# A two-layer hybrid encoder trunk: longer allowances in the clock that orders attention and projection work

## Chip, core and metric

The kernel runs on one core of one Trainium2 chip. A core has a matrix engine (TensorE, PE in the profile; PEld is its weight load), a vector engine (VectorE, DVE), an engine for activation functions and scaled copies (ScalarE, ACT), a general engine (GpSimd, POOL) and an engine that here issues the transfers (SyncE, SP). Each takes its own instructions strictly in the order in which the program lists them, and waits at an instruction until what it needs is there. The metric is the time of one execution on the device in microseconds, as the median of several runs.

## What is computed

Two layers over 512 tokens of width 1024. The attention of each layer has two branches that matter here, eight heads each: latent attention ("mla") and grouped-query attention ("gqa", eight query heads over two key heads of width 64).

```python
for l in range(DEPTH):                      # DEPTH = 2, SEQ = 512, D_MODEL = 1024
    h = rms_norm(x, attn_norm_g[l])
    proj = h @ w_in[l]
    c_q, c_kv, k_rope, gq, gk, gv, pool_in, gate_logits = split_columns(proj, IN_SIZES)
    o_mla = mla_branch(c_q, c_kv, k_rope, ...)      # 8 heads, keys of width 96, values of 64
    o_gqa = gqa_branch(gq, gk, gv, ...)             # 8 heads over 2 key heads, width 64
    o_pool = pool_branch(pool_in, pool_w[l], pool_scale[l])
    gates = sigmoid(gate_logits).reshape(b, s, 3, d)
    merged = (gates[:, :, 0] * (o_mla @ w_branch_mla[l])
              + gates[:, :, 1] * (o_gqa @ w_branch_gqa[l])
              + gates[:, :, 2] * (o_pool @ w_branch_pool[l]))
    x = x + merged @ w_out[l]
    hf = rms_norm(x, ffn_norm_g[l])
    u = depthwise_conv(hf @ ffn_w_up[l], ffn_conv_w[l], ffn_conv_b[l])
    x = x + (silu(u[..., :D_FF]) * u[..., D_FF:]) @ ffn_w_down[l]
```

Each head does `softmax(q k^T / sqrt(d)) v`.

## The kernel before

Everything stays on one core, and activations lie feature by feature: 128 features of all 512 tokens are one tile. A product in float32 is made of three matmuls on rounded halves (`mm3`): high by high, high by low, low by high. A 512-wide matmul of a 128x128 block is the unit of PE's work.

**Filler.** The gate and branch projections and the latent heads' own projections are cut into pieces of three or more matmuls. A `Filler` hands them out one by one (`fill.step()`), always in the same order. They need little from other engines, so they are put between the steps of the heads, which wait for other engines often.

**Banks.** PSUM is cut into eight banks: two each for `acc`, `ST` and `AV`, one each for `S` and `mi`. Taking one is `ps(tag)`, giving it back is `free(tag)`, which notes the time from which it counts as free.

**The ordering clock.** The program's order is not written down by hand. While it is being written out, a small clock (`Clock`, object `ck`) keeps a time for every engine from estimated costs: `ck.now` is the time at which PE stands, `ck.ready[key]` the time from which a result counts as there, and the numbers in `banks[tag]` those from which a bank is free. No such time is in the finished program; they decide only which instruction is listed next. On the chip, semaphores do the waiting, whatever the clock thought.

**Grouped-query heads** (`PLAN["gqa"]`). A fixed plan gives each step of the eight heads a place in the stretch of filler. The steps of a head are: `t_q` (its queries are cut into high and low), four `s_max` (a rough score block, 128 queries by 512 keys, in the single bank `S`, whose row maximum DVE takes; the bank is free when DVE has read it), four `probs` (the scores that are used, from two matmuls into a bank `ST` or `mi`, then exponential on ACT, high and low parts on ACT and DVE, and a partial sum on DVE, after which the bank is free), then `av_hi`, `av_lo` and `av_rest` (the product with the values). Before a step is listed, filler is listed up to the place that the plan gives, and after that more filler, piece by piece, as long as `waiting` says that a key or bank of the step is not there yet, to at most `SLACK` = 35 pieces ahead of the place.

**Latent heads** (`held_banks`). Here a list of tasks is gone through again and again, and the first that may go is listed (`can`); if none may, a piece of filler is. `a_part` makes a score block's first matmul into any bank that `sc_ready` finds free, and DVE takes its maximum (`largest`); after the fourth, DVE joins the maxima and writes a row of them (`row`) into the operand `qb`, which counts as key `m`. `b_part` adds the two other matmuls, the second of which reads `qb`, and the exponential follows. A task's `margin` is how long its keys must have been there by the clock.

In the listings below, `ps_S<-ka,qa` is an `s_max`, `ps_ST<-qa,ka` and `ps_ST<-qb,kb` (or `ps_mi`) a `probs`, `ps_AV<-ph`, `<-pl` and `<-vt` the three products with the values, `ps_ST<-qa,kh` (or `mi`, `S`, `AV`) an `a_part`, `<-qa,kl` and `<-qb,kh` a `b_part`, and `ps_acc` filler.

Of the kernel before, what the change touches and what calls it, by code (L numbers as in the profile page):

```python
# [60 lines left out]
D_OUT, D_IN, D_LAT = 3.2, 4.0, 6.0  # L61
D_FREE, D_SUM = 0.8, (2.0, 0.8)
REST = 0.4
GAP = 3.0
ONLY = True
HOLD = (0.65, 0.15)
# [93 lines left out]
class Clock:  # L160
# [49 lines left out]
    def done(self, *key):  # L210
        self.ready[key] = self.fin + self.SEM
# [10 lines left out]
    def chain(self, *steps, after=0.2):  # L222

        def go(n, source=None, since=None):
            if n == len(steps):
                return
            keys, fn = steps[n] if isinstance(steps[n], tuple) else ((), steps[n])
            late = [self.ready.get(k, self.now + 0.5) for k in keys]
            if late and max(late) > self.now:
                self.at(max(late) - self.now, lambda: go(n))  # L230
                return
            if fn in self.waits and self.pause[0] <= self.now < self.pause[1] - 0.001:
                self.at(self.pause[1] - self.now, lambda: go(n, source, since))
                return
            eng, most = self.gives_way.get(fn, (None, 0.0))
            since = self.now if since is None else since
            if self.free.get(eng, 0.0) > self.now + 0.02 and self.now < since + most:
                self.at(self.free[eng] - self.now, lambda: go(n, source, since))
                return
            self.fin, self.source, self.last = self.now, source, None  # L240
            fn()
            source, self.source = self.last, None
            self.at(max(0.0, self.fin - self.now), lambda: go(n + 1, source))
        self.at(after, lambda: go(0))
# [74 lines left out]
def trunk(ctx: ExitStack, tc: tile.TileContext, x, w, prm, gb, cst, pad, out):  # L319
    nc = tc.nc  # L320
    ctx.enter_context(tc.manual_schedule())
    ck = Clock()
# [30 lines left out]
    banks = {k: [0.0] * n for k, n in nbank.items()}  # L353
# [172 lines left out]
    for l in range(L):  # L526
        t = cp.tile([P, NPRM], F32, tag=f"prm{l}", name=f"prm{l}")
        prms.append(t)

    def split(hi, lo, src, scale=None, eng=None):  # L530

        steps = []
        if scale is None:
            steps.append(lambda: A.activation(hi, src, AF.Copy))
            steps.append(lambda: (eng or V).tensor_tensor(lo, src, f(hi), ALU.subtract))
        else:
            steps.append(lambda: A.activation(hi, src, AF.Copy, scale=scale))
            steps.append(lambda: V.scalar_tensor_tensor(lo, src, scale, f(hi), ALU.mult, ALU.subtract))
        return steps
# [128 lines left out]
    def layer(l, sq, xsrc):  # L668
# [616 lines left out]
        def attention(kind, fill, okey, odst):  # L1285
            gqa = kind == "gqa"
            hs, ot = {}, []

            def key(*k):
                return (kind, l) + k  # L1290
# [3 lines left out]
            def sc_tags():  # L1294
                return ("ST", "mi", "S") + ("AV",) * (held[0] == 0)

            def sc_ready():
                return any(banks[t] and banks[t][0] <= ck.now for t in sc_tags())

            def sc_bank():  # L1300
                while not any(banks[t] for t in sc_tags()):
# [288 lines left out]
            def held_banks():  # L1590
                todo = []

                def task(fn, *args, keys=(), margin=0.2, bank=None, after=(), fills=0.0):
                    todo.append((fn, args, keys, margin, bank, after, fills))

                lead, late = LEAD[kind]
                step = (fill.total - fill.done - late) / 7.0
                f0 = fill.done
                issued = set()
                for h in range(8):  # L1600
                    if not gqa and h + 1 < 8 or gqa and h in (1, 3, 5):
                        n = h + 1
                        task(go_turn, n, after=[(a_part, h - 1, 3)] if not gqa and h else [(a_part, h, 0)] if gqa else ())
                    q = [("gqn", l, b) for b in range(4)] if gqa and h == 0 else [("tp" if gqa else "tq", l, h)]
                    if not gqa or h % 2 == 0:
                        task(t_q, h, keys=q, bank="mi" if gqa and h == 0 else None, after=[(a_part, h - 1, 3)] if h else ())
                    if not gqa:
                        task(t_k, h, keys=[("tk", l, h)], after=[(t_q, h)])
                    for k in range(4):
                        task(a_part, h, k, keys=[key("q" if gqa else "qh", h)] + [key("kh", h)] * (not gqa), margin=0.1, bank="sc",  # L1610
                             after=[(t_q, h - h % 2 if gqa else h)] + [(b_part, h - 1, 3)] * (h > 0) + [(t_k, h)] * (not gqa)
                             + [(a_part, h, k - 1)] * (k > 0), fills=f0 + step * h if k == 0 else 0)
                    for k in range(4):
                        task(b_part, h, k, keys=[key("m", h), key("q", h)] + [key("kl", h)] * (not gqa), margin=0.4,
                             after=[(b_part, h, k - 1) if k else (a_part, h, 3)])
                    for k in range(4):
                        task(av_hi, h, k, keys=[key("ph", h, k)], margin=lead, bank="AV" if k == 0 else None,
                             after=[(av_hi, h, k - 1) if k else (b_part, h, 0), (b_part, h, k)] + [(av_rest, h - 1)] * (h > 0))
                        task(av_lo, h, k, keys=[key("pl", h, k)], margin=lead,
                             after=[(av_hi, h, k)])  # L1620
                    task(av_rest, h, keys=[key("t", h, 3)], margin=lead, after=[(av_lo, h, k) for k in range(4)])

                def can(fn, args, keys, margin, bank, after, fills):
                    if not all(x in issued for x in after):
                        return False
                    if fills and fill.done < min(fills, fill.total):
                        return False
                    if not all(ck.ready.get(k, 1e9) + margin <= ck.now for k in keys):
                        return False
                    if bank == "sc":  # L1630
                        return sc_ready()
                    return not bank or bool(banks[bank]) and banks[bank][0] <= ck.now

                while todo:
                    for n, z in enumerate(todo):
                        if can(*z):
                            todo.pop(n)
                            z[0](*z[1])
                            issued.add((z[0],) + z[1])
                            break  # L1640
                    else:
                        if not fill.step():
                            ck.to(ck.now + 0.05)
                fill.finish()
# [6 lines left out]
            for h in range(8):  # L1651
# [4 lines left out]
                for k in range(4):  # L1656
                    plan += [(p0 + s0 + ds * k, s_max, (h, k)), (p0 + 4 + k, probs, (h, k)),
                             (p0 + 4 + k + ah, av_hi, (h, k)), (p0 + 4 + k + al, av_lo, (h, k))]
                plan.append((p0 + 7 + al + REST, av_rest, (h,)))
            plan.sort(key=lambda z: z[0])  # L1660
# [4 lines left out]
            def waits(fn, h, k=None):  # L1665

                if fn is go_turn:
                    return [], None
                if fn is t_q:
                    if gqa and h == 0:  # L1670
                        return [("gqn", l, b) for b in range(4)], "mi"
                    return [] if gqa and h % 2 else [("tp" if gqa else "tq", l, h)], None
                if fn is t_k:
                    return [("tk", l, h)] * (not gqa), None
                if fn is s_max:
                    return [key("q", h)] + [key("kh", h)] * (not gqa), "S"
                if fn is probs:
                    return [key("m", h), key("q", h)] + [key("kl", h)] * (not gqa), ("ST", "mi")
                if fn is av_hi:
                    return [key("ph", h, k)], "AV" if k == 0 else None  # L1680
                return [key("t", h, 3)] if fn is av_rest else [key("pl", h, k)], None

            def waiting(fn, *args):
                keys, tag = waits(fn, *args)
                tags = (tag,) if isinstance(tag, str) else tag or ()
                return not ck.has(*keys) or bool(tags) and not any(banks[t] and banks[t][0] <= ck.now for t in tags)

            f0, first = fill.done, plan[0][0]
            for pos, fn, args in plan:
# [51 lines left out]
        tags = ("acc", "ST", "AV", "mi", "S")  # L1741
# [212 lines left out]
        def again(k):  # L1954

            turned[k] = [slot("tf", F32R)[:, :T] for _ in range(4)]
            for i, (src, hi, lo, key_) in enumerate((
# [3 lines left out]
                SY.dma_start(t, src)  # L1961
                chain(*split(hi, lo, t, eng=G), lambda key_=key_: done(*key_), after=D_IN + GAP * i + 3.0 * (k == 0))

# [312 lines left out]
```

## Time and profile before

| what | value |
|---|---|
| time, median of 3 runs | 1524.32 us (1524.0 to 1524.4) |
| the profiled execution's own time | 1525.42 us |
| its span, from first to last instruction | 1523.6 us, 25155 instructions |
| read from HBM, written | 159.89 MB, 22.02 MB |
| layer 0: grouped-query heads, latent heads | 104 to 216 us, 218 to 343 us |
| layer 1: the same | 860 to 972 us, 974 to 1098 us |

The last two rows are stretches of the trace that hold those heads; the rest of a layer is projections and the feed-forward part. Three kinds of view are used below: the busy time of each engine in a stretch, what PE's weight load waited for, and the timeline of an engine, in which a row's first two numbers are its start and its length in us. Matmuls overlap in the pipeline: a row is longer than the distance from its start to the next one's, and it is this distance that tells how fast PE goes. What stands between brackets is idle time that even the overlap doesn't hide.

### The profile page before, as it was taken

To read this page: it belongs to the slowest core of one execution; us is meant where nothing else is said; L and a number is where in the kernel's file an instruction comes from. 1 tells how busy PE (TensorE), PEld (TensorE's weight loads), DVE (VectorE), ACT (ScalarE), POOL (GpSimd) and SP (SyncE) were. 2 spreads that over 40 slices of the span, in tenths; PEclk is the share of its full clock that TensorE was granted. 3 is DMA by queue.
4 is the path that set the end of the run, shared out by engine and by line. 5 is a ranking of instruction groups with operands and counts; after the bars stand their busy time and mean duration, and the time that the engine had idled before them with its cause. 6 is when DMAs were issued, how large, how long until landed. Compare 5 with 4: busy or idle time off the path is not lost.

```text
span 1523.6 us, 25155 instructions
## 1 busy us (share of the span) xinstructions
PE 1513.9 (99%) x8390; PEld 1326.5 (87%) x8390; DVE 1188.6 (78%) x2375; ACT 980.0 (64%) x1973; POOL 1121.2 (74%) x1076
## 2 busy tenths in 40 slices
PE   9999999999999999999999999999999999999998
PEld 8888788788889899999998888888888899989998
DVE  5778989985578885778857789899855788867786
ACT  6468876664567675666654688676636676756763
POOL 4865986865689897676778659868547897977664
PEclk9999999999999999999999999999999999999999
DMA  6432234424244453233435322444243444533232
GB/s 219 116 116 79 66 106 139 130 88 148 96 136 145 149 185 110 92 101 108 140 127 135 101 77 67 124 132 133 78 152 97 142 149 139 182 109 100 96 114 95
DMA packets 91954, 183.56 MB, mean 120 GB/s; under 512 B 21936, under 2 KB 43696, under 8 KB 91824
## 3 DMA queue, kind: packets, MB, share of 16 engines
q1 hardware_dynamic: 91680, 181.94, 37.9%
q8 instruction: 66, 1.08, 0.3%
q14 instruction: 64, 0.52, 0.1%
q10 hardware_dynamic: 144, 0.01, 0.0%
HBM read 159.89 MB, written 22.02 MB: 119 GB/s over the span
## 4 chain that ended last, share of the span: by engine, by line
PE 89%; DVE 5%; ACT 2%; issue 1%; DMA 1%; POOL 1%; SPq 0%; DVEq 0%; POOLq 0%; ACTq 0%
PE ps_acc L497 29%; PE ps_AV L497 18%; PE ps_ST L497 10%; PE ps_ST L1927 10%; PE ps_acc L1927 9%; PE ps_AV L1927 7%; PE ps_S L497 2%; PE ps_mi L497 2%; DVE nmt L295 1%; DVE vt L289 1%; DVE pl L285 1%; PE ps_ST L1467 1%; DMA tf<-pad 0%; DVE ph L303 0%; ACT wh L277 0%
## 5 line engine op out<-in xcount | busy, mean ns | idle before, releaser
L285 POOL TENSOR_TENSOR wl<-raw,wh 128x512 fp32r<-128x512 f32 (+3 forms) x500 | 594.1, 1197 | 288.0 <-ACT wh L277 236.5
L277 ACT ACTIVATE wh<-raw 128x512 fp32r<-128x512 f32 (+2 forms) x521 | 291.2, 577 | 18.1 <-PE ps_ST L497 10.4
L497 PE MATMUL ps_acc<-HH,wh 128*128 128x512 f32 x504 | 197.0, 391 | 0.0
L497 PE MATMUL ps_acc<-HL,wh 128*128 128x512 f32 x504 | 196.5, 390 | 0.0
L497 PE MATMUL ps_acc<-HH,wl 128*128 128x512 f32 x504 | 196.4, 390 | 0.0
L497 PEld LDWEIGHTS ps_acc<-HH,wl 128*128 128x128 f32 x504 | 94.6, 188 | 20.0
L497 PEld LDWEIGHTS ps_acc<-HL,wh 128*128 128x128 f32 x504 | 94.7, 188 | 19.1
L497 PEld LDWEIGHTS ps_acc<-HH,wh 128*128 128x128 f32 x504 | 94.7, 188 | 18.9 <-DVE gt L285 0.6
L497 PE MATMUL ps_AV<-HH,wh 128*128 128x512 f32 x248 | 96.7, 390 | 0.0
L497 PE MATMUL ps_AV<-HL,wh 128*128 128x512 f32 x248 | 96.6, 390 | 0.0
L497 PE MATMUL ps_AV<-HH,wl 128*128 128x512 f32 x248 | 96.6, 389 | 0.0
L277 ACT ACTIVATE wh<-ps_S 128x512 fp32r<-128x512 f32 x79 | 47.1, 597 | 40.4 <-DVE ps_S L285 28.6
L277 ACT ACTIVATE wh<-ps_mi 128x512 fp32r<-128x512 f32 x79 | 47.1, 596 | 38.4 <-DVE ps_mi L285 32.4
L285 DVE TENSOR_TENSOR wl<-ps_mi,wh 128x512 fp32r<-128x512 f32 x79 | 54.1, 685 | 11.4 <-ACT wh L277 10.8
L285 POOL TENSOR_TENSOR a<-a,cv 128x511 f32<-128x511 f32 x36 | 46.1, 1294 | 22.6 <-DVE a L289 22.6
L285 DVE TENSOR_TENSOR wl<-ps_S,wh 128x512 fp32r<-128x512 f32 x79 | 54.1, 685 | 9.9 <-ACT wh L277 9.3
L1927 PE MATMUL ps_ST<-ah,wh 128*128 128x256 f32 x298 | 59.8, 283 | 0.2 <-ACT wh L277 0.2
L277 ACT ACTIVATE gt<-gt 128x512 f32<-128x512 f32 x48 | 30.2, 628 | 43.5 <-DVE gt L285 43.1
L497 PEld LDWEIGHTS ps_AV<-HH,wl 128*128 128x128 f32 x248 | 46.6, 188 | 9.8
L1927 PE MATMUL ps_acc<-ah,wh 128*128 128x256 f32 x276 | 55.0, 283 | 0.0
L497 PEld LDWEIGHTS ps_AV<-HH,wh 128*128 128x128 f32 x248 | 46.6, 188 | 9.3
L497 PEld LDWEIGHTS ps_AV<-HL,wh 128*128 128x128 f32 x248 | 46.6, 188 | 9.3
(583 smaller groups left out, 5173.4 us busy)
## 6 DMA issues: line engine op xcount, KB each, us to landing
raw<-w SPq DMA_DIRECT2D x228, 512.0 KB, 3.6
raw<-w SPq DMA_DIRECT2D x13, 384.0 KB, 3.0
XM<-x SPq DMA_DIRECT2D x16, 256.0 KB, 3.2
back<-hsp SPq DMA_DIRECT2D x16, 256.0 KB, 4.1
back<-tsp SPq DMA_DIRECT2D x16, 256.0 KB, 4.4
dtq<-tr SPq DMA_DIRECT2D x16, 192.0 KB, 1.9
dtk<-tr SPq DMA_DIRECT2D x16, 192.0 KB, 2.0
tf<-dtq SPq DMA_DIRECT2D x48, 64.0 KB, 2.0
```

The costliest lines, as they stand in the source:

```text
L277: return self.eng.activation(out, in_, func, **k)
L285: return self.eng.tensor_tensor(out, *a)
L289: return self.eng.scalar_tensor_tensor(out, *a)
L295: return self.eng.tensor_reduce(out, in_, *a, **k)
L497: PE.matmul(o, lhsT=lhsT, rhs=rhs, start=start, stop=stop)
L1467: PE.matmul(sc, lhsT=s[a_][:, kb_], rhs=s[b_][:, :T], start=False, stop=n == len(pairs) - 1, skip_group_check=True)
L1927: PE.matmul(banks_[b][1][:, 256 * at_:256 * at_ + 256], lhsT=(his, his, los)[q][i][:, ws], rhs=right[n][q == 1], start=first and b not in ...
```

## The change

Three conditions get longer allowances, all of them in the ordering clock.

```diff
+LATE = (0.3, 0.3)
...
             def sc_ready():
-                return any(banks[t] and banks[t][0] <= ck.now for t in sc_tags())
+                return any(banks[t] and banks[t][0] + 0.5 <= ck.now for t in sc_tags())
...
                     for k in range(4):
-                        task(b_part, h, k, keys=[key("m", h), key("q", h)] + [key("kl", h)] * (not gqa), margin=0.4,
+                        task(b_part, h, k, keys=[key("m", h), key("q", h)] + [key("kl", h)] * (not gqa), margin=0.8,
...
             def waiting(fn, *args):
                 keys, tag = waits(fn, *args)
                 tags = (tag,) if isinstance(tag, str) else tag or ()
-                return not ck.has(*keys) or bool(tags) and not any(banks[t] and banks[t][0] <= ck.now for t in tags)
+                return any(ck.ready.get(k, 1e9) + LATE[0] > ck.now for k in keys) or \
+                    bool(tags) and not any(banks[t] and banks[t][0] + LATE[1] <= ck.now for t in tags)
```

In the grouped-query heads a step's keys and bank count as there only 0.3 us after the time that the clock has for them. In the latent heads a bank for `a_part` counts as free 0.5 us after, and the keys of `b_part` must have been there for 0.8 us instead of 0.4.

On PE both programs have the same instructions. Filler moves to earlier places and the heads' steps to later ones, by 24 matmuls at most, inside the two stretches of each layer; the last product of the last head of each kind stands behind the same amount of filler in both. Three places follow.

The first is on PE, in layer 0's grouped-query heads, between the first and the second `s_max` of head 6 (operands `qa_2071` before, `qa_2104` now). Before, the end of that piece:

```order
L497 MATMUL ps_AV_2041<-ph_2035,vg_591 128x512
L497 MATMUL ps_AV_2041<-pl_1950,vg_589 128x512
L497 MATMUL ps_acc_2057<-HH,wh_2013 128x512
L497 MATMUL ps_acc_2057<-HL,wh_2013 128x512
L497 MATMUL ps_acc_2057<-HH,wl_2014 128x512
L497 MATMUL ps_S_2148<-ka_595,qa_2071 128x512
```

and now its end:

```order
L498 MATMUL ps_acc_2203<-opl_919,wh_2038 128x512
L498 MATMUL ps_acc_2203<-oph_918,wl_2039 128x512
L498 MATMUL ps_acc_2203<-oph_925,wh_2038 128x512
L498 MATMUL ps_acc_2203<-opl_926,wh_2038 128x512
L498 MATMUL ps_acc_2203<-oph_925,wl_2039 128x512
L498 MATMUL ps_acc_2203<-oph_934,wh_2038 128x512
L498 MATMUL ps_acc_2203<-opl_935,wh_2038 128x512
L498 MATMUL ps_acc_2203<-oph_934,wl_2039 128x512
L498 MATMUL ps_acc_2203<-oph_952,wh_2038 128x512
L498 MATMUL ps_acc_2203<-opl_953,wh_2038 128x512
L498 MATMUL ps_acc_2203<-oph_952,wl_2039 128x512
L498 MATMUL ps_S_2227<-ka_595,qa_2104 128x512
```

Between the two `s_max` stood two products with the values and 6 filler matmuls; now it is the same two products and 15 filler matmuls.

The second is on PE, in layer 0's latent heads, where the last score block of head 3 is taken between the products with the values of head 2. Before:

```order
L497 MATMUL ps_AV_3209<-ph_3176,vm_2545 128x512
L1425 MATMUL ps_mi_3224<-qa_3088,kh_3091 128x512
L497 MATMUL ps_AV_3209<-pl_3170,vm_2543 128x512
L1425 MATMUL ps_S_3228<-qa_3088,kh_3091 128x512
L1425 MATMUL ps_AV_3231<-qa_3088,kh_3091 128x512
L1425 MATMUL ps_ST_3234<-qa_3088,kh_3091 128x512
```

and now:

```order
L498 MATMUL ps_AV_3212<-pl_3171,vm_2539 128x512
L1426 MATMUL ps_AV_3239<-qa_3091,kh_3094 128x512
L498 MATMUL ps_acc_3241<-oh_1775,wh_3098 128x512
L498 MATMUL ps_acc_3241<-ol_1776,wh_3098 128x512
L498 MATMUL ps_acc_3241<-oh_1775,wl_3099 128x512
L498 MATMUL ps_AV_3212<-pl_3177,vm_2541 128x512
L498 MATMUL ps_acc_3241<-oh_2116,wh_3098 128x512
L498 MATMUL ps_acc_3241<-ol_2117,wh_3098 128x512
L498 MATMUL ps_acc_3241<-oh_2116,wl_3099 128x512
L1426 MATMUL ps_ST_3256<-qa_3091,kh_3094 128x512
```

The four `a_part` of head 3 stood nearly together; now 7 other matmuls stand between the third and the fourth alone.

The third is on DVE, the chain of maxima of the same head 3 (the four `nmt` of 128x16 are the maxima of the four blocks, `mrow` and `qb` end the chain). Before:

```order
L295 TENSOR_REDUCE nmt_3226<-ps_mi_3224 128x16
L289 SCALAR_TENSOR_TENSOR vt_3191<-ps_ST_3080,vm_131_1030,vt_3191 128x512
L295 TENSOR_REDUCE nmt_3226<-ps_S_3228 128x16
L295 TENSOR_REDUCE nmt_3226<-ps_AV_3231 128x16
L295 TENSOR_REDUCE nmt_3226<-ps_ST_3234 128x16
L295 TENSOR_REDUCE nmt_3226<-nmt_3226 128x16
L311 STREAM_TRANSPOSE osum_2967<-oinv_3124 128x512
L295 TENSOR_REDUCE nmt_3226<-nmt_3226 32x16 x3
L285 TENSOR_TENSOR gt_3260<-ps_acc_3135,rbc_374 128x512
L295 TENSOR_REDUCE mrow_3271<-nmt_3226 32x16
L285 TENSOR_TENSOR qb_3089<-mrow_3271,C 32x512
```

and now:

```order
L296 TENSOR_REDUCE nmt_3222<-ps_AV_3239 128x16
L290 SCALAR_TENSOR_TENSOR vt_3200<-ps_ST_3083,vm_131_1030,vt_3200 128x512
L286 TENSOR_TENSOR gt_3237<-ps_acc_3134,rbc_374 128x512
L312 STREAM_TRANSPOSE osum_2967<-oinv_3127 128x512
L296 TENSOR_REDUCE nmt_3222<-ps_ST_3256 128x16
L296 TENSOR_REDUCE nmt_3222<-nmt_3222 128x16
L296 TENSOR_REDUCE nmt_3222<-nmt_3222 32x16 x3
L296 TENSOR_REDUCE mrow_3293<-nmt_3222 32x16
L290 SCALAR_TENSOR_TENSOR gt_2689<-gt_2689,ps_acc_3241 128x512
L286 TENSOR_TENSOR qb_3092<-mrow_3293,C 32x512
```

The transpose of `osum` and the gate's `gt<-ps_acc` stood inside the chain, behind the fourth maximum; now they stand ahead of it, and another piece of the gates stands ahead of `qb`.

## The prediction

> **What bounds the kernel now.** I read the page first, for the engine that sets the end.
>
> ```profile
> PE 1513.9 (99%) x8390; PEld 1326.5 (87%) x8390; DVE 1188.6 (78%) x2375; ACT 980.0 (64%) x1973; POOL 1121.2 (74%) x1076
> PEclk9999999999999999999999999999999999999999
> ```
>
> PE is busy for 99% of the span at the full granted clock. The change adds and removes no matmul, so it can win only what PE now waits, and lose only by new waits. Next come the four stretches that hold the heads, as busy time by engine.
>
> ```profile
> core 0: us, PE busy (x) PEld busy (x) DVE busy (x) ACT busy (x) POOL busy (x), PEclk, DMA share, GB/s
> 104.00:216.00 112.00, 110.86 (x506) 91.30 (x505) 96.70 (x175) 87.70 (x174) 82.81 (x114) 1.00 0.23 75
> 218.00:343.00 125.00, 124.32 (x550) 101.69 (x549) 114.85 (x211) 81.35 (x152) 87.70 (x75) 1.00 0.42 125
> 860.00:972.00 112.00, 111.17 (x507) 91.66 (x506) 96.30 (x176) 89.22 (x175) 81.83 (x113) 1.00 0.23 75
> 974.00:1098.00 124.00, 123.67 (x546) 100.89 (x545) 114.68 (x211) 80.53 (x152) 86.78 (x74) 1.00 0.42 127
> ```
>
> PE's plain idle time there is 1.14 + 0.68 + 0.83 + 0.33 = 3.0 us. That is too little, since a matmul's row lasts longer than its turn, and a short wait hides under the row before. The reader is to see also that DVE is the second engine: 86% in the first and third stretch, 92% in the others. The waits show fully at the weight load, which stands ahead of each matmul. Of the view of waits over the whole span, with the engine PEld, these rows belong to the heads' stretches:
>
> ```profile
> PEld ps_S L497 <- DVE nm L295: 4.7, 8, 1.0
> PEld ps_ST L1425 <- DVE vt L289: 2.0, 4, 0.7
> PEld ps_acc L497 <- DVE gt L285: 1.8, 4, 0.6
> PEld ps_mi L1467 <- DVE qb L285: 0.7, 1, 0.7
> PEld ps_acc L497 <- DVE XM L289: 0.7, 2, 0.4
> PEld ps_acc L497 <- ACT MQ L277: 0.6, 1, 0.6
> PEld ps_S L497 <- ACT qb L277: 0.4, 1, 0.4
> PEld ps_AV L1467 <- DVE qb L285: 0.3, 1, 0.3
> PEld ps_ST L1467 <- DVE qb L285: 0.2, 1, 0.2
> ```
>
> The columns are total us, times, longest. The largest group is a rough score block that waits for the only bank `S`, because DVE has not yet read the block before (`nm`). The next is a latent score block that waits for a bank which DVE's partial sum `vt` still reads, and the three `qb` rows are score parts that wait for the row of maxima. What such a wait costs is read from one of the two longest.
>
> ```profile
> 178.91 0.39 PE L497 MATMUL ps_acc<-HH,wl 128*128 128x512 f32 x1
> 179.86 0.50 PE L497 MATMUL ps_S<-ka,qa 128*128 128x512 f32 x1 [0.56 <-DVE nm L295]
> 180.20 0.39 PE L497 MATMUL ps_ST<-qa,ka 128*128 128x512 f32 x1
> ...
> 176.10 2.39 DVE L285 TENSOR_TENSOR qa<-tf,qa 64x512 fp32r<-64x512 f32 x2
> 178.52 0.69 DVE L295 TENSOR_REDUCE ssm<-mns 128x8 f32<-128x512 f32 x1
> 179.13 0.68 DVE L295 TENSOR_REDUCE nm<-ps_S 128x1 f32<-128x512 f32 x1
> ```
>
> The usual pitch is taken where nothing waits:
>
> ```profile
> 130.85 0.39 PE L497 MATMUL ps_ST<-qa,ka 128*128 128x512 f32 x1
> ...
> 132.90 0.39 PE L497 MATMUL ps_acc<-oph,wh 128*128 128x512 f32 x1
> ```
>
> From the first to the last of these rows are nine matmuls: 2.05 / 9 = 0.23 us each. At 179.86 the distance is 0.95, so 0.72 is lost, and the next distance is 0.34, so 0.11 more: 0.83 us, where the weight load's wait is 1.0 (the longest of its group). I take 0.83 of a weight-load wait as its cost. The `S` group then costs 4.7 x 0.83 = 3.9 us, `vt` and `qb` together 3.2 x 0.83 = 2.7, and the four groups that remain 3.5 x 0.83 = 2.9.
>
> **The change part by part.** No semaphore, transfer or tile size is changed. The three conditions move filler forward and steps back, so each edit's price is a cover longer or shorter by so many matmuls of 0.23 us.
>
> Grouped-query heads, 0.3 more for keys and banks. The clock moves in pieces of three matmuls, 0.68 us, so a step that was just due gets one piece or more. I looked up the eight places of the `S` group in both orders. At four the cover grows. In head 6 of either layer it goes from 8 to 17 matmuls, 2.0 us more than the 0.83 that was lost. At 127.77 it goes from 8 to 11 and at 155.79 from 8 to 14 (six of them 256 wide, so about 0.7 us more):
>
> ```profile
> 126.99 0.39 PE L497 MATMUL ps_acc<-HH,wl 128*128 128x512 f32 x1
> 127.77 0.50 PE L497 MATMUL ps_S<-ka,qa 128*128 128x512 f32 x1 [0.39 <-DVE nm L295]
> 128.10 0.39 PE L497 MATMUL ps_mi<-qa,ka 128*128 128x512 f32 x1
> ...
> 155.26 0.39 PE L497 MATMUL ps_acc<-oph,wl 128*128 128x512 f32 x1
> 155.79 0.50 PE L497 MATMUL ps_S<-ka,qa 128*128 128x512 f32 x1
> 156.13 0.40 PE L497 MATMUL ps_mi<-qa,ka 128*128 128x512 f32 x1
> ...
> 934.46 0.39 PE L497 MATMUL ps_acc<-HH,wl 128*128 128x512 f32 x1
> 935.41 0.50 PE L497 MATMUL ps_S<-ka,qa 128*128 128x512 f32 x1 [0.57 <-DVE nm L295]
> ```
>
> The losses there are 0.55 + 0.10 = 0.65, then 0.30 + 0.11 = 0.41, and 0.72 + 0.11 = 0.83 in layer 1. With the first 0.83 that is 2.7 us, less than the added cover at each place, and I count it as gone. At the other four places the cover stays within 0.05 us of what it was; their 3.9 - 2.7 = 1.2 us stays. At four places that are not among the eight (the second gap of head 4, and in layer 1 the third gap of head 1 and the last two of head 4) the cover shrinks by three matmuls, 0.68. That costs between nothing and 0.68 at each; since none of them waited, some of the cover was spare, and I take a third, 0.23, together +0.9 us.
>
> Latent heads, banks 0.5 later and `b_part` at 0.8. Their waits look like these:
>
> ```profile
> 269.42 0.39 PE L1425 MATMUL ps_AV<-qa,kh 128*128 128x512 f32 x1
> 270.06 0.50 PE L1425 MATMUL ps_ST<-qa,kh 128*128 128x512 f32 x1 [0.26 <-DVE vt L289]
> 270.40 0.39 PE L497 MATMUL ps_acc<-HH,wh 128*128 128x512 f32 x1
> ...
> 276.81 0.40 PE L1467 MATMUL ps_mi<-qa,kl 128*128 128x512 f32 x1
> 277.44 0.50 PE L1467 MATMUL ps_mi<-qb,kh 128*128 128x512 f32 x1 [0.23 <-DVE qb L285]
> 277.77 0.40 PE L1467 MATMUL ps_S<-qa,kl 128*128 128x512 f32 x1
> ...
> 275.59 1.79 DVE L285 TENSOR_TENSOR qb<-mrow,C 32x512 fp32r<-32x512 f32 x1
> ```
>
> They lose 0.41 + 0.11 and 0.40 + 0.10 us. In the new order 7 matmuls, 1.6 us, stand ahead of that fourth score block, and two long pieces have left its chain of maxima, for one that came in. The parts are spread, so three of the four maxima are taken before the last block comes, while from the fourth block to `b_part` the distance hardly changes (4.8 to 6.1 us of matmuls now, 4.8 to 6.4 before). An allowance of 0.5 covers a wait of 0.5, and the longest here is 0.7 at the weight load. I count 80% of 2.7 as gone: -2.1 us; the bounds are none of it and all of it.
>
> Not addressed: the waits for `gt`, `XM`, `MQ` and ACT's `qb`, 2.9 us. They are waits for an `acc` bank or a copy that no allowance looks at. They fall anew with another order, up or down, and I take nothing. Filler at earlier places also needs its weights earlier, by up to 24 matmuls or 5.4 us. The projections outside the heads take weights at PE's full pace all along, and the heads' stretches hold filler for only part of the time, so I price it at nothing; if POOL and ACT failed to keep up, it would show as a wait for `wh` or `wl`, up to the 1.8 us of the largest group that is not addressed. The transfers are the same 594, a few in another order. Both kinds of heads end behind the same matmul as before, so the stages behind them move by the sum and no more.
>
> The sum: -2.7 + 0.9 - 2.1 = -3.9 us. The profiled execution would go from 1525.4 to 1521.5 us, its span from 1523.6 to 1519.7. It lies 1.1 us above the median of the runs, to which I apply the same step: 1524.3 - 3.9 = **1520.4 us**.
>
> **The rivals.** First, the waits come back elsewhere, because the clock's errors are longer than the allowance. Behind 179.86 and 277.44 stand two DVE pieces with both inputs in SBUF that took far longer than usual, as the view by tile shows for one of them (shortest, median, longest in ns):
>
> ```profile
> L285 DVE TENSOR_TENSOR qa<-tf,qa x4: 686/907/1673, 123.8 to 176.8; 64x512 fp32r<-64x512 f32 x4
> ```
>
> The stretch is 1.67 - 0.69 = 0.98 us, and an allowance of 0.3 leaves 0.68. Such pieces fall beside other POOL work in the new order, and two more 512-wide splits of filler weights go to DVE in place of two 256-wide ones. Four new hits behind which PE stands would cost 2.7 us: 1520.4 + 2.7 = 1523.1, no change that can be told. Against it: the clock charges DVE for some of these collisions already, and in head 6 there is cover for a whole stretch. [...] Chance 0.24.
>
> Second, slower: the bunch. Where filler was spent early, the plan is ahead of its place, and now lists steps with no filler between: two `probs`, four products with the values and the sum's product stand in a row, ten new times over both layers (end of heads 2 to 6). Each `probs` needs a bank that DVE gives back after its fourth piece; if DVE is late, nothing covers it. At the worst loss seen, 0.83 each, this is +8.3, so 1520.4 + 8.3 = 1528.7 us; it decides for slower from 0.70 each. Against it: the row from 130.85 to 132.90 quoted above is just such a bunch, in head 1, and ran at full pitch. Chance 0.12.
>
> Third, the change does nothing measurable, since every gain is met by a loss at the shortened places (4 x 0.68 = 2.7) and the waits that are not addressed grow by half of their 2.9: -4.8 + 2.7 + 1.4 = -0.7, or 1523.6 us. Chance 0.10; it ends on the same side as the first.
>
> **How the numbers follow.** Forecast 0.54, rivals 0.24, 0.12 and 0.10. A measurement of this kernel can tell about 0.2%, 3 us, from no change: faster is below 1521.3, slower above 1527.4. The forecast's own spread is 1518.5 to 1521.8, and a part of it, 0.02, lies above the bound; a small part of the other cases, 0.04, falls below it. So faster 0.56, same 0.33, slower 0.11. The range goes down to all of the `S`, `vt` and `qb` waits gone with no new one, 1524.3 - 6.6 = 1517.7, and up past the first and third rival to a bunch at half its worst price, 1520.4 + 4.2, rounded up to 1525.0.
>
> **What would show it.** In the trace after, PEld's waits for `nm` should fall from 4.7 to about 2 us, with none in head 6 of either layer; those for `vt` and `qb` from 3.2 to under 1; the four groups that are not addressed should stay near 3.5. PE busy in the four stretches should come nearer to their length, and DVE keep its sum. It is wrong if new waits for `ST` or `mi` banks stand in the bunches, if waits for `wh` or `wl` appear in the heads, or if the time falls although the `nm` row doesn't.

## The result, and the profile after

The change made the kernel slower: 1528.62 us (median of 10 runs, 1528.1 to 1529.97) against 1524.41 for the kernel before beside it (10 runs, 1523.67 to 1525.8), a ratio of 1.0028 [1.002, 1.0036]. The forecast was 1520.4. The span of the profiled execution went from 1523.6 to 1527.1 us. One execution of a kernel further down (DVE relieved, in the order of before) took 3885 us and was the profiled one: its ratio leaves it out, and no trace of that kernel is shown.

The first view is the busy time by engine in the same four stretches, after the change (columns as above).

```profile
104.00:216.00 112.00, 109.55 (x499) 89.97 (x498) 95.11 (x171) 83.85 (x169) 79.87 (x109) 1.00 0.24 75
218.00:343.00 125.00, 124.60 (x552) 102.10 (x550) 115.75 (x217) 82.19 (x154) 89.17 (x76) 1.00 0.42 124
860.00:972.00 112.00, 109.39 (x493) 88.86 (x493) 95.19 (x167) 86.51 (x170) 79.44 (x108) 1.00 0.25 78
974.00:1098.00 124.00, 123.91 (x550) 102.03 (x549) 115.18 (x218) 83.03 (x157) 90.14 (x80) 1.00 0.43 128
```

The clock is 1.00 throughout. In the latent stretches PE is busier than before (124.60 for 124.32, 123.91 for 123.67), in the grouped-query stretches less (109.55 for 110.86, 109.39 for 111.17). The two halves of the change went opposite ways, which the start of one and the same matmul tells in us: the product that ends layer 0's grouped-query heads starts at 219.82 instead of 217.71, so these heads lost 2.1; the latent heads behind them then took 1.0 less (343.34 instead of 342.21 at their end). In layer 1 the loss is 3.2 and the gain 0.9.

What PE's weight load waited for in layer 0's grouped-query heads (104 to 221 us), before and then after:

```profile
PEld ps_S L497 <- DVE nm L295: 3.1, 5, 1.0
PEld ps_acc L497 <- DVE XM L289: 0.2, 1, 0.2
```

```profile
PEld ps_ST L498 <- ACT qb L278: 1.7, 2, 1.0
PEld ps_acc L498 <- DVE XM L290: 1.5, 1, 1.5
PEld ps_AV L498 <- ACT ph L278: 0.9, 2, 0.6
PEld ps_acc L498 <- DVE MK L304: 0.9, 1, 0.9
PEld ps_S L498 <- DVE nm L296: 0.7, 2, 0.5
PEld ps_AV L498 <- DVE vt L290: 0.5, 1, 0.5
PEld ps_AV L498 <- DVE pl L286: 0.2, 1, 0.2
```

And in layer 1 (860 to 979 us), before and after:

```profile
PEld ps_S L497 <- DVE nm L295: 1.6, 3, 1.0
PEld ps_acc L497 <- ACT MQ L277: 0.6, 1, 0.6
PEld ps_acc L497 <- DVE XM L289: 0.4, 1, 0.4
PEld ps_S L497 <- ACT qb L277: 0.4, 1, 0.4
```

```profile
PEld ps_S L498 <- DVE nm L296: 2.0, 5, 0.8
PEld ps_acc L498 <- ACT MK L278: 1.5, 1, 1.5
PEld ps_acc L498 <- DVE XM L290: 1.5, 2, 0.8
PEld ps_ST L498 <- ACT qb L278: 0.6, 1, 0.6
PEld ps_ST L498 <- DVE vt L290: 0.6, 1, 0.6
PEld ps_AV L498 <- DVE vt L290: 0.4, 1, 0.4
PEld ps_acc L498 <- ACT wh L278: 0.4, 1, 0.4
```

The `nm` row, at which the change aimed, did fall, from 4.7 to 2.7 over both layers. All the others together rose from 1.6 to 10.7; half of that is filler that waits for its own bank (the `ps_acc` rows with `XM`, `MQ` or `MK`, pieces that read that bank), from 1.2 to 5.4. The sum went from 6.3 to 13.4; 7.1 more at the weight load, times the 0.83 of the prediction, is 5.9 us, where the starts above say 2.1 + 3.2 = 5.3. By the engine waited for, ACT's rows grew from 1.0 to 5.1 and DVE's from 5.3 to 8.3.

Two of the new waits, at their place. The first is filler waiting for its own bank: PE's timeline, and DVE's behind which the bank's reader `XM` stood.

```profile
153.68 0.39 PE L498 MATMUL ps_acc<-HH,wl 128*128 128x512 f32 x1
155.13 0.38 PE L498 MATMUL ps_acc<-wh,cth 128*128 128x256 f32 x1 [1.07 <-DVE XM L290]
```

```profile
152.94 0.70 DVE L290 SCALAR_TENSOR_TENSOR vt<-ps_mi,vg,vt 128x512 fp32r<-128x512 f32 x1
153.68 0.69 DVE L286 TENSOR_TENSOR qa<-tf,qa 64x512 fp32r<-64x512 f32 x1
154.39 0.69 DVE L290 SCALAR_TENSOR_TENSOR XM<-gt,ps_acc 128x512 f32<-128x512 f32 x1
```

No DVE row here has idle time before it in brackets (nor have the nine rows ahead, back to 148.48): the queue is full, `XM` stands behind the others in it, and PE, nine filler matmuls into a run, needs the bank that `XM` reads. The second is a `probs` that waits for the row of maxima, on PE and on ACT:

```profile
196.22 0.39 PE L498 MATMUL ps_ST<-qa,ka 128*128 128x512 f32 x1
197.22 0.50 PE L498 MATMUL ps_ST<-qb,kb 128*128 128x512 f32 x1 [0.61 <-ACT qb L278]
```

```profile
195.90 1.26 ACT L278 ACTIVATE qb<-nmt 32x128 fp32r<-32x128 f32 x4
```

ACT wrote all four pieces of the row one behind the other, 1.26 us, and ended at 197.16. In the latent heads, on the other hand, the rows shrank; in layer 0 (222 to 344 us, where before had 2.6: `vt` 1.0, `gt` 0.9, `qb` 0.7) there are left:

```profile
PEld ps_ST L1426 <- DVE vt L290: 0.5, 1, 0.5
PEld ps_AV L498 <- DVE vt L290: 0.5, 1, 0.5
PEld ps_acc L498 <- DVE gt L286: 0.3, 1, 0.3
PEld ps_acc L498 <- DVE gt L290: 0.2, 1, 0.2
```

### The profile page after: what moved, and what is told of

It reads as the page before. It is cut to its first block, busy times and chain, and to the rows that moved or that the text cites. A ratio compares the mean times of both kernels' runs of the same rounds, so it can differ in the third digit from the quotient of the medians.

```text
span 1527.1 us, 25167 instructions
## 1 busy us (share of the span) xinstructions
PE 1515.0 (99%) x8390; PEld 1326.8 (87%) x8390; DVE 1187.0 (78%) x2378; ACT 976.4 (64%) x1970; POOL 1119.9 (73%) x1076
## 4 chain that ended last, share of the span: by engine, by line
PE 84%; DVE 6%; POOL 4%; ACT 3%; issue 1%; DMA 1%; SPq 0%; POOLq 0%; DVEq 0%; ACTq 0%
PE ps_acc L498 26%; PE ps_AV L498 17%; PE ps_ST L1929 10%; PE ps_ST L498 9%; PE ps_acc L1929 9%; PE ps_AV L1929 7%; PE ps_S L498 2%; PE ps_mi L498 2%; POOL wl L286 1%; DVE vt L290 1%; DVE pl L286 1%; DVE nmt L296 1%; POOL MQ L286 1%; POOL oraw L286 1%; PE ps_ST L1468 1%
```

## The experiments

Each ratio is against runs of the kernel before beside it; where a difference in us is given, it is that of the two medians. "Span" is that of the profiled execution (before: 1523.6).

### The halves of the change

First the change was taken apart. Grouped-query heads alone (latent lines as before):

```diff
-                return any(banks[t] and banks[t][0] + 0.5 <= ck.now for t in sc_tags())
+                return any(banks[t] and banks[t][0] <= ck.now for t in sc_tags())
...
-    margin=0.8,
+    margin=0.4,
```

> Only the grouped-query part of the change (0.3 for keys and banks there); the latent heads have their old allowances. Theory bunch (filler spent ahead leaves the heads' steps in a row, and DVE and ACT then hold up PE): all of the loss and more, since the latent part gained 1.9 us in the trace: slower than before by 5 to 6 us, 1529.5 to 1530.5. Rival (the latent allowances or the filler's earlier weights are behind it): less than the 4.2 us of the whole change.

1529.78 us, ratio 1.004 [1.0027, 1.0052]: +5.8. Latent heads alone (`LATE = (0.0, 0.0)`):

> Only the latent part of the change (0.5 for banks, margin 0.8). By the trace of the whole change the latent stretches became 0.98 and 0.92 us shorter: faster than before by about 1.9 us, 1522.5. Rival (the latent gain was a consequence of the other order in the grouped-query heads): no change within 0.7 us of before.

1522.86 us, ratio 0.9992 [0.9984, 1.0001]: -1.1, its span 2.7 less. The halves have the signs that the stretches show, though the interval of the second just includes no change. Then the two parts of the grouped-query half by themselves, latent heads as before: keys alone (`LATE = (0.3, 0.0)`)

> Only the grouped-query part, and of it only the keys' 0.3; banks count as free at the clock's own time. Its order has one run of nine or more head steps without filler per layer, as before. Theory bunch: no loss, within 1 us of before. Rival (any allowance shifts work against POOL or the filler's banks, keys and banks alike): about half of the loss of both together, +2 to +3 us.

and banks alone (`LATE = (0.0, 0.3)`)

> Only the grouped-query part, and of it only the banks' 0.3. Its order has six and four runs of nine or more head steps without filler (before: one and one; whole change: six and six). Theory bunch: most of the loss, +3 to +5 us, with the waits for the S bank (nm) mostly gone all the same. Rival (keys and banks alike): about half of the loss, +2 to +3 us.

Keys 1527.53 us, 1.0024 [1.0015, 1.0034], +3.6; banks 1527.01 us, 1.0023 [1.0013, 1.0033], +3.0. So the theory of the bunch fell in its first form: the keys' order has no more bunches than before and loses as much.

### Dose, direction, and an order moved for no reason

With the latent heads as before, the allowance was halved, doubled and turned round, and in a fourth kernel only the plan's end was nudged.

```diff
-LATE = (0.3, 0.3)
+LATE = (0.15, 0.15)
```

> Latent heads as before, the allowance of the grouped-query heads 0.15 for keys and banks instead of 0.3 (the steps stand 10 to 15 filler matmuls later than before, at 0.3 they stood 17 to 23 later and lost 5.8 us). Theory A, filler ahead is what costs, and more of it costs more: about half, +2 to +4 us. Theory B, the order before is one that fits the chip and any other order of the same steps loses, whatever its direction: no dose, anything from +1 to +7, and not ordered between this run, 0.3 and 0.6.

```diff
-LATE = (0.3, 0.3)
+LATE = (0.6, 0.6)
```

> Latent heads as before, the allowance 0.6 for keys and banks (steps 36 to 39 filler matmuls later, so the cap of 35 pieces is still far). Theory A: +9 to +13 us. Theory B: the same as 0.3 within 3 us, +3 to +9; and if an allowance of 0.6 at last exceeds the errors of the ordering clock, waits for nm fall below 2 us and the time may even come back to before.

```diff
-LATE = (0.3, 0.3)
+LATE = (-0.3, -0.3)
```

> Latent heads as before, the allowance -0.3: keys and banks count as there 0.3 before the clock's time, so steps stand 2 to 6 filler matmuls earlier than before, about as far as the keys' allowance alone moved them the other way (1 to 3), for a loss of 3.6. Theory A: filler is less ahead, so acc and MQ/MK waits fall and nm waits grow: 0 to +3, by nm alone (18 to 24 of 32 score blocks stand one or two pieces, 0.7 us, earlier). Theory B: +2 to +6, with waits in all the groups.

```diff
-PLAN = {"gqa": (-4.2, -1.0, -0.2, 0.0, 0.65, 2.411, 4.57, 32.003)}
+PLAN = {"gqa": (-4.2, -1.0, -0.2, 0.0, 0.65, 2.411, 4.57, 31.7)}
...
-LATE = (0.3, 0.3)
+LATE = (0.0, 0.0)
```

> Latent heads and all allowances as before, only the end of the plan is put at 31.7 instead of 32.003, so the steps stand 4 to 5 filler matmuls later on average, half of them not at all. No rule of waiting is changed. Theory A: no loss, 0 to +1, since filler is hardly ahead of the plan (the plan moves with it). Theory B: +2 to +5, as for the keys' allowance alone, which moved as little.

| allowance or plan | us | ratio | against before |
|---|---|---|---|
| -0.3 | 1528.55 | 1.0027 [1.0016, 1.0038] | +4.2 |
| 0.15 | 1531.34 | 1.0049 [1.0036, 1.0061] | +7.0 |
| 0.3 | 1529.78 | 1.004 [1.0027, 1.0052] | +5.8 |
| 0.6 | 1543.46 | 1.0128 [1.0113, 1.0144] | +19.1 |
| 0, plan's end at 31.7 | 1527.11 | 1.0018 [1.0009, 1.0027] | +2.8 |

Up to 0.3 there is no dose and no direction, as theory B had it: half the allowance lost no less than the whole, a negative one lost too, and so did a nudge of the plan. In the nudged kernel the aimed-at `nm` row halved, and the loss came from elsewhere:

```profile
PEld ps_S L498 <- DVE nm L296: 2.3, 5, 0.8
...
PEld ps_ST L498 <- POOL qb L286: 1.8, 2, 0.9
PEld ps_ST L498 <- ACT qb L278: 1.5, 2, 0.9
```

At 0.6 a second thing is added, outside both theories' ranges: filler runs out. The last 24 matmuls of the heads had none between them (8 before), and PE stood still for the head's own chain: two waits for `vt`, one in each layer, of up to 2.9 us at the weight load.

### A cap on how far filler runs ahead

```diff
-SLACK = 35
+SLACK = 8
```

> Latent heads as before, the grouped-query heads' allowance of 0.3 as in the change, but filler may stand only 8 pieces ahead of the plan instead of 35. The steps then stand 2 to 6 filler matmuls later instead of 17 to 23, no run of filler is longer than 12, and the end of the heads is as before. If the loss of 5.8 us is that of filler far ahead of the plan: 0 to +2 us. If any other order than the fitted one loses 3 to 7: +3 to +7 again.

1531.35 us, 1.0045 [1.0032, 1.0059]: +6.8. Filler far ahead of the plan is not what costs. With the steps only 2 to 6 matmuls off, the waits for `nm` came more often than before, and others with them:

```profile
PEld ps_S L498 <- DVE nm L296: 6.6, 18, 0.7
...
PEld ps_S L498 <- ACT qb L278: 2.2, 2, 1.1
```

### One wait covered, and little else moved

The prediction's largest term was head 6. Here the allowance holds at its second score block alone, with the latent half kept (a few neighbours in head 6 move with it, as the expectation says), and then at three places.

```diff
-                return any(ck.ready.get(k, 1e9) + LATE[0] > ck.now for k in keys) or \
-                    bool(tags) and not any(banks[t] and banks[t][0] + LATE[1] <= ck.now for t in tags)
+                late = LATE[1] if fn is s_max and args == (6, 1) else 0.0
+                return not ck.has(*keys) or bool(tags) and not any(banks[t] and banks[t][0] + late <= ck.now for t in tags)
```

> Latent heads as in the change, and in the grouped-query heads the allowance of 0.3 holds only for the bank of the second score block of head 6, the place of the two longest waits (0.83 us each). Three score blocks and two probs in each layer stand 3 to 6 filler matmuls later, everything else stands where it stood before. The latent part alone measured -1.1 us (its span -2.7). If the prediction's pricing of a place is right, -1.7 more: a span about 4.4 us under that of before, no nm wait in head 6. If any other order of the grouped-query heads loses (theory B), even these two places give nothing or cost: a span no better than 2.7 under, with new waits within the next few us of 180 and 935.

```diff
-                late = LATE[1] if fn is s_max and args == (6, 1) else 0.0
+                late = LATE[1] if fn is s_max and args in ((4, 3), (5, 3), (6, 1)) else 0.0
```

> As the run with one place, and the same allowance also at the last score blocks of heads 4 and 5, where before lost 0.41, 0.30 and 0.27 us. By the prediction's pricing 0.4 to 0.8 us better than with one place (the last block of head 4 moves by three matmuls in both layers, that of head 5 not at all). By theory B no better, or 1 to 2 us worse.

One place: 1522.51 us, 0.9989 [0.998, 0.9998], span 1521.8. Three places: 1523.25 us, 0.9994 [0.9986, 1.0003], so the two further places gained nothing that shows. PE's timeline with one place:

```profile
179.24 0.50 PE L498 MATMUL ps_S<-ka,qa 128*128 128x512 f32 x1
179.58 0.39 PE L498 MATMUL ps_ST<-qa,ka 128*128 128x512 f32 x1
...
181.20 0.39 PE L498 MATMUL ps_acc<-HH,wl 128*128 128x512 f32 x1
181.76 0.50 PE L498 MATMUL ps_S<-ka,qa 128*128 128x512 f32 x1 [0.18 <-DVE nm L296]
182.10 0.40 PE L498 MATMUL ps_AV<-ph,vg 128*128 128x512 f32 x1
```

The span is 1.8 under that of before, not 4.4. The second score block (179.24) starts without a stop, and only 0.11 is still lost in the distance behind it (0.34). The third (181.76) now stops: 0.56 - 0.23 = 0.33, and 0.11 behind it, in a place that lost nothing before; the same in layer 1. Of 0.83 there is left 0.11 + 0.33 + 0.11 = 0.55, so the two places gained 2 x 0.28 = 0.56 us. The medians fit that (-1.7, where the latent half alone had -1.1), but the intervals overlap, and the span of the latent half alone was lower still, 2.7 under before. The two traces show where the gain went: the latent heads stand in the same order in both, yet behind the earlier grouped-query heads they took 0.49 us longer in layer 0 and 0.54 in layer 1, by the starts of the products that end the two kinds of heads (layer 0: 217.24 and 340.57 with the latent half alone, 216.91 and 340.73 here). So waits are dealt anew even where no instruction changes its place; with one trace of each it is not shown that this holds for every execution. The busy time of before over these 14 us fits the part of the wait that only moved:

```profile
174.00:188.00 14.00, 13.44 (x66) 11.00 (x65) 13.82 (x22) 11.91 (x23) 13.73 (x14) 1.00 0.21 68
```

DVE is busy for 13.82 of 14: while its queue has no gap, cover ahead of one block moves the wait to the next. The next kernel covers the whole head.

```diff
-                late = LATE[1] if fn is s_max and args == (6, 1) else 0.0
+                late = {(6, 1): 0.3, (6, 2): 1.0, (6, 3): 1.0}.get(args, 0.0) if fn is s_max else 0.0
```

> Latent heads as in the change; in head 6 alone the allowance is 0.3 for the bank of the second score block and 1.0 for those of the third and fourth, so that the lateness of 0.34 us that the run with one place found at the third block meets three more filler matmuls. If lateness is passed from block to block and only cover over the whole head takes it away: nm waits in head 6 gone, about 0.7 us (two layers) better than with one place, a span of 1521.1 or less. If the wait moves on once more (to the row of maxima, to acc, or to a probs): no better than 1521.8, with a new wait at 184 to 192 and 939 to 947.

1522.51 us, 0.9988 [0.9979, 0.9997], span 1520.7. Head 6 stops no more, but head 7, 12 us later, does, where the kernel with one place lost 0.11 only:

```profile
193.59 0.39 PE L498 MATMUL ps_acc<-HH,wl 128*128 128x512 f32 x1
194.02 0.50 PE L498 MATMUL ps_S<-ka,qa 128*128 128x512 f32 x1
```

The distance is 0.43 for a usual 0.23, with 0.11 more behind it. The span is 1.1 better, the median the same, so the runs can't tell whether anything was won over the single place. Both are faster than before by about 0.1%, the best of the kernels that compute the whole sum, but not told apart from the latent half alone.

### The latent half, taken apart and enlarged

Grouped-query heads as before. The bank's 0.5 alone:

```diff
-    margin=0.8,
+    margin=0.4,
```

> Grouped-query heads as before; of the two edits in the latent heads only the bank's 0.5, b_part at its old 0.4. By the prediction's reading most of the 3.2 us at the weight load are vt (2.0), a wait for banks, so two thirds of the latent gain or more should come with this half: a span 1.5 to 2.7 us under that of before. If the gain is that of b_part, or of the two together, the span is within 1 us of before.

`b_part`'s margin alone:

```diff
-                return any(banks[t] and banks[t][0] + 0.5 <= ck.now for t in sc_tags())
+                return any(banks[t] and banks[t][0] <= ck.now for t in sc_tags())
```

> Grouped-query heads as before; of the two edits in the latent heads only b_part's margin of 0.8, the bank's allowance at zero. The bank's half alone measured +0.9 and both together -1.1. If the two add: -2 us. If the gain hangs on the order that the two make together: between -1 and +2, with vt waits in other places than before.

Both, and longer:

```diff
-                return any(banks[t] and banks[t][0] + 0.5 <= ck.now for t in sc_tags())
+                return any(banks[t] and banks[t][0] + 0.8 <= ck.now for t in sc_tags())
...
-    margin=0.8,
+    margin=1.2,
```

> Grouped-query heads as before; the latent heads' allowances longer than in the change: a bank 0.8 (for 0.5), b_part 1.2 (for 0.8). If an allowance of 0.5 left waits of up to 0.7 that a longer one covers, 0 to 1 us better than the latent part alone (-1.1 to -2): -1.5 to -3. If a longer allowance costs as in the grouped-query heads, it gives the gain back: -0.5 to +3, with the latent stretches 1 to 2 us longer.

Bank alone 1525.14 us, 1.0006 [0.9997, 1.0015], +0.9; `b_part` alone 1529.42 us, 1.0031 [1.0019, 1.0042], +4.8; together, above, -1.1; longer 1534.58 us, 1.0068 [1.0055, 1.008], +10.3. The parts don't add (0.9 + 4.8 for a measured -1.1), and `b_part` alone and the longer allowances lie outside what either theory expected: each makes an order of its own. With `b_part` alone (and with the longer allowances) too little filler is left at the end, and the last product waits for its partial sum, once in each layer (the group in the view of waits, then PE's timeline in layer 0):

```profile
PEld ps_AV L498 <- DVE vt L290: 4.7, 2, 2.3
```

```profile
340.76 0.39 PE L498 MATMUL ps_AV<-pl,vm 128*128 128x512 f32 x1
343.05 0.50 PE L498 MATMUL ps_AV<-vt,unit 128*128 128x512 f32 x1 [1.90 <-DVE vt L290]
...
345.14 0.63 PE L498 MATMUL ps_acc<-HH,wh 128*128 128x512 f32 x1
345.56 0.63 PE L498 MATMUL ps_acc<-HL,wh 128*128 128x512 f32 x1
```

By the distances the two waits lost 2.06 us each, and 1.6 more was lost behind the first (last section): 5.7 with `b_part` alone, more than its whole +4.8. So its loss lies at the end of the heads, and the rest of its order lost nothing.

### DVE relieved, under three fixed orders

The last theory was that the new orders lose because they run into DVE's full queue. The partial sums of the grouped-query heads were cut to a quarter of their columns (the rest of the sum is left out), while the ordering clock still charged the whole. PE's order stays word for word that of before, of 0.3, and of the nudged plan; latent heads as before.

```diff
-                        V.scalar_tensor_tensor(t, sc, vals(h, k)[1], f(t),
-                                               ALU.mult, ALU.add)
+                        if gqa:
+                            V._two(t, ins=(sc, f(t)))
+                            V.eng.scalar_tensor_tensor(t[:, :P], sc[:, :P], vals(h, k)[1], f(t[:, :P]), ALU.mult, ALU.add)
+                        else:
+                            V.scalar_tensor_tensor(t, sc, vals(h, k)[1], f(t), ALU.mult, ALU.add)
```

> Order of before, word for word on PE; only DVE's 48 partial sums vt of the grouped-query heads work on 128 of the 512 columns (the other columns of the partial sums keep the first block's part; the ordering clock still charges the whole). That takes some 0.4 us each, 10 us a layer, off DVE and nothing off PE. Theory D, PE's waits there are a DVE with a full queue (99% busy from 174 to 188): the waits of 1.5 to 2.5 us a layer in these heads mostly go, -2 to -4 us. If they are only a matter of order and latency: -1 to 0.

> The same relief of DVE with the order of the allowance of 0.3 in the grouped-query heads alone, which lost 5.8 us against before. Theory D: most of the 5.8 goes, since XM, MK and nm no longer stand behind a full queue; what is left are the waits for ACT's and POOL's qb: +0 to +2 over the run with the order of before and the same relief. If the order itself is what costs, whatever DVE's queue: still +4 to +6 over that run.

> The same relief with the order of the nudged plan (31.7), which lost 2.8 us against before. Theory D: within 1 us of the run with the order of before and the same relief, or up to +1.5 by its qb waits (ACT, POOL), which the relief doesn't touch. If the order itself costs: +2 to +3.5 over it.

Order of before 1521.78 us, 0.9983 [0.9974, 0.9992], -2.6; order of 0.3: 1528.45 us, 1.0026 [1.0016, 1.0035]; order of the nudge: 1525.39 us, 1.0008 [0.9999, 1.0017]. Against before these are -2.6, +4.1 and +1.1, so the relief was worth 2.6 in the first, 1.7 in the second (from +5.8) and 1.7 in the third (from +2.8): DVE's load does stretch the waits. But the distance between the orders stayed: 6.7 us (5.8 without relief) and 3.6 (2.8). This theory fell too. In the relieved order of 0.3 the waits for `XM` were less than half of the 3.0 after the change, while those for ACT's `qb` and `MK` (2.3 and 1.5 there) stood unchanged:

```profile
PEld ps_ST L498 <- ACT qb L278: 2.3, 3, 1.0
...
PEld ps_acc L498 <- ACT MK L278: 1.5, 1, 1.5
PEld ps_acc L498 <- DVE XM L290: 1.3, 2, 0.9
```

## Why the prediction was wrong

**What bounds the kernel: right.** PE is busy for 99% of either span, and all that moved was its waits. The price of 0.83 for each us at the weight load held roughly: 7.1 x 0.83 = 5.9, for 5.3 by the starts in the same trace and +5.8 for the grouped-query half alone.

**The four covered places, -2.7: three of four, and the sum right by luck.** Head 6's second block in both layers and the place of 127.77 wait no more; the last block of head 4 in layer 0 (155.79 before, 163.09 after) still waits, 0.54 at the weight load, in spite of its longer cover. The four places that were to keep their 1.2 us lost it, and six that had not waited do now: the longest, 0.79, at head 2's second block in layer 1 (888.39), and one, 0.29, in head 6 (third block in layer 1, 948.85), where none was expected. So the group fell to 2.7, near the 2 forecast, but largely at other places. And a covered wait is not a saved one. After the change PE waits just ahead of head 6 instead, twelve filler matmuls into a run, for its own bank: 0.9 for DVE's `MK` (181.53) and 1.5 for ACT's (939.81). With only head 6's place moved, 0.28 of each 0.83 was saved and the rest met the next block; with the whole head covered, head 7 had some of it.

**The four shortened places, +0.9: less.** One of them waited in the trace, and lost 0.38 us (head 4 of layer 1, at 917.31).

**"Not addressed ... I take nothing": this step failed.** It said that the waits for `XM`, `MQ`, ACT's `qb` and the like fall anew with another order, up or down, and priced them at zero on average. In the grouped-query heads all groups but `nm` went from 1.6 to 10.7 at the weight load, some 7.5 us. Up and down were not equally likely: the order before had only 1.6 of them left to lose. The largest part is filler's waits for its own bank (1.2 to 5.4): the cover itself waits. Eight other orders of these heads that were not confined to one or three places were run (allowances of -0.3, 0.15, 0.3 and 0.6, keys alone, banks alone, cap, nudge), and all eight lost, by 2.8 to 19.1 us.

**Filler's earlier weights, nothing: nearly right.** In the grouped-query heads one wait for `wh`, 0.4 at the weight load, is all that appeared, and none for `wl`.

**The latent heads, -2.1: right in size, on shaky ground.** The stretches gained 1.0 + 0.9, while the half alone measured -1.1 by its median. The rows for `qb` are gone and `vt` stayed at 2.0 (half of it now before the product with the sums); the rest of the gain came from `gt`, which had been priced at nothing (1.8 to 0.8). The bank's edit alone shows no gain, and `b_part`'s alone loses by two waits at the very end; that points to this one order, not to the allowance as such.

**The rivals.** The slower one named the right number, 1528.7, by luck, for a wrong reason: it put the loss at `ST` and `mi` banks in bunches without filler, and one such wait appeared, 0.41 us at 970.43. The keys' order lost with no more bunches than before (one of nine or more matmuls in each layer), and the order of -0.3 lost with none in its trace. The stretched DVE pieces of the first rival are there (`qa<-tf,qa` took 1.61 us at 938.54, for 0.69 at 153.68; a POOL piece ran beside the long one from 938.33 to 939.60, and what holds such a piece up was not shown), but a lighter DVE did not close the gap. The third had the right idea, that gains are met by waits that aren't addressed, with a fifth of their size.

What stays open is why the order before fits so well. That it was better than these eight neighbours is shown; whether its plan's numbers, fitted anew under a longer allowance, would do as well was not tried.

## What to carry to other kernels

When a scheduler's rule is changed, everything after it is dealt anew, and the waits that the old order had already got rid of come back: price the groups of waits that are now near zero as a loss, not as zero (here, in the grouped-query heads, they went from 1.6 to 10.7 us). Read first whether the engine waited for has idle time at that place; if it has none, expect cover to move the wait to the next piece (here DVE was busy for 13.82 of 14 us, and cover ahead of one block saved 0.28 of its 0.83). Change one place with the rest held, and compare the trace place by place: a gain of half a microsecond here was too small for the medians to show.

## What had not been expected of the hardware

A long wait cost more than its length. In the kernel with `b_part` alone PE stood from 340.76 to 343.05, a matmul's turn included; five matmuls later the distance became 0.40 to 0.43 instead of 0.23, eight times over (the last two rows of the timeline above are two of these). The granted clock, the last number but two, in 3 us behind this wait and behind its twin in layer 1:

```profile
345.00:348.00 3.00, 3.00 (x9) 2.28 (x9) 2.31 (x4) 1.29 (x4) 1.41 (x1) 0.54 0.06 8
...
1104.00:1107.00 3.00, 3.00 (x15) 2.49 (x14) 2.41 (x5) 1.29 (x4) 1.42 (x1) 1.00 0.62 180
```

At 0.54 there were 9 matmuls in 3 us for 15, and 8 x 0.2 = 1.6 us lost beside the 2.06 of the wait (343.05 - 340.76 - 0.23). Behind the wait of the same length in layer 1 the clock stayed at 1.00, so it doesn't always come. In the kernel with an allowance of 0.6, PE stood from 217.56 to 220.39 in layer 0, 2.6 us beside a matmul's turn, and from 221.04 on the distance was 0.42 to 0.43, seven times over; the mean clock of its two latent stretches (218 to 343 and 974 to 1098 us) was 0.99, for 1.00 before the change. With `b_part` alone a pause of 2.3 us was enough in layer 0 and as long a one was not in layer 1; what decides it was not shown.
